# Branch A's ScalarE and VectorE instructions in an order written by hand for all tiles

## The chip, the core and the metric

The kernel runs on one core of one Trainium2 chip. The core's engines are TensorE (PE in the profile, its weight loads PEld), VectorE (DVE), ScalarE (ACT), GpSimd (POOL) and SyncE (SP, which here issues the DMAs). Each runs its own stream of instructions, and they meet at semaphores. The metric is the device time of one execution in microseconds; less is better.

## The reference

One encoder block over 1024 tokens and 16 prepended meta tokens, width 1024: two attention branches side by side, merged by sigmoid gates, then a SwiGLU feed-forward layer. All is float32. Branch A, where the change lies, is differential attention with 4 heads:

```python
s1 = jnp.einsum('bqhd,bkhd->bhqk', q1, k1).astype(jnp.float32) * scale + bias
s2 = jnp.einsum('bqhd,bkhd->bhqk', q2, k2).astype(jnp.float32) * scale + bias
attn = jax.nn.softmax(s1, axis=-1) - lam * jax.nn.softmax(s2, axis=-1)
return jnp.einsum('bhqk,bkhe->bqhe', attn.astype(v.dtype), v)
...
merged = jax.nn.sigmoid(ga) * (y_a @ w_ba) + jax.nn.sigmoid(gb) * (y_b @ w_bb)
```

`bias` is minus the head's slope times the distance of query and key. The gates `ga` and `gb` are two 1024 x 1024 projections of the normed input.

## The kernel before

Every float32 product is made of three matmuls on a high and a low part (`split`, lines 117 and 118: ACT rounds the high part out, DVE or POOL subtracts it to get the low one). Work runs in stages: norm and projections with branch B, then branch A, then the branch outputs, the output projection and the feed-forward layer.

**Branch A** goes over 4 heads of 8 query tiles of 128 rows, 32 tiles in all, numbered `n` from 0 (`h, t = divmod(n, NT)`; the text calls the heads 1 to 4). For each tile there are two maps, first `m = 1`, then `m = 0`, each of 1040 keys in three chunks of 392, 392 and 256 (`scores_a`). So a tile has six chunks: per chunk two matmuls (line 814) into one of five score banks, and one DVE instruction (line 817) that adds the distances, keeps the scores in the map and the running minimum. After a map's third chunk ACT takes the exponential with the sum (line 824). DVE takes the reciprocal of the sum (line 826), POOL scales map 1 by it and by minus lambda (line 828). The join is DVE's `scalar_tensor_tensor` (line 837), map 0 times its reciprocal plus map 1, with a small copy behind it (line 838).

A tile's joined map is turned during the next tile (`T_LAG` is 1): three groups of transposes on TensorE (line 849: four, four and one) into the same five banks, each followed by an ACT copy (line 852) and a DVE subtraction (line 853). Two tiles together go through `values_a` (line 862) in three steps, four tiles through `normed_a`.

**The gates** fill TensorE between these: `gate_steps` has 50 units (products `p` of a Strassen-like scheme, column groups `k`), each of four steps of three matmuls (line 751), in two banks. The result of a unit is added to a kept sum on DVE (line 756) for p = 1, 6 and 7 or copied out on ACT (line 759) for the others, and stored. The first 18 units are all copies. The last 32 take p = 1, 6, 7, 4 in turn, for two k each. The weights of a unit are loaded (`g_load`) and split (`g_split`) three units ahead by `g_ahead`.

**The order.** TensorE's order is by hand (`order_pe`). A string gives the slots of a tile: `s` a chunk, `g` a gate step, `t` a group of transposes of the tile before, `n` a step of values or norm:

```python
SLOTS = "sgsgsngsgsstntnt"
...
for what in SLOTS if n != 1 else "sgsgsngsgssggtntnt":
```

At the start of a head stand more gate steps, 10 (`G_HEAD`), 4 for the first (`G_FIRST`). ACT and DVE are held to program order in tile 0 alone (`order_first`); there, splits wait in `held_back` until `let_go`. From tile 1 on a scheduler with costs of its own orders ACT and DVE. In program order each exponential stands behind its map's last chunk and the join at the end of the tile's slots. POOL and SP are ordered by the scheduler in this stage.

Of the kernel before, what the change touches and what calls it, by code (L numbers as in the profile page):

```python
# [9 lines left out]
F32 = mybir.dt.float32  # L10
# [3 lines left out]
AF = mybir.ActivationFunctionType  # L14
# [5 lines left out]
P = 128  # L20
# [7 lines left out]
AH = 4  # L28
# [8 lines left out]
N_WAIT = 3  # L37
PP2 = 2
# [35 lines left out]
def encoder_block(ctx: ExitStack, tc: tile.TileContext, x, meta, norm_mix, w_in, lq1, lk1, lq2, lk2,  # L74
# [666 lines left out]

    def gate_steps():
        for n, (p, k) in enumerate(order_g):
            g_ahead(n + 1)
            op, act = g_ready.pop((p, k)), G_ACT[p]
            if p in (2, 5, 1):
                g_bank[k] = pp_bank(f"pg{p}_{k}")
            ps = g_bank[k]
            for c in range(4):
                for i, (a, b) in enumerate(((0, 0), (0, 1), (1, 0))):  # L750
                    nc.tensor.matmul(ps, op[:, a, c], quad(b, *act)[:, c], start=(p in (2, 5, 1) and c == 0 and i == 0),  # L751
                                     stop=(p in (2, 3, 4) and c == 3 and i == 2), skip_group_check=True)
                if c == 3:
                    if p in (1, 6, 7):
                        st = g_kept.pop((p, k))
                        nc.vector.tensor_tensor(st, ps, st, ALU.add)  # L756
                    else:
                        st = gpool.tile([P, 512], F32, tag="g", name="gate_stage", bufs=G_BUFS)
                        nc.scalar.copy(st, ps)
                    nc.sync.dma_start(g_place(p, k), st)  # L760
                    if (p, k) in ((5, 3), (5, 7), (3, 7)):
                        later_p = {(5, 3): 6, (5, 7): 7, (3, 7): 4}[p, k]
                        load_sums(later_p, *G_ACT[later_p])
                yield
# [34 lines left out]
    behind_first, n_tile = [], [0]  # L799

    def scores_a(h, t, ld, s):
# [5 lines left out]
        u0 = 896 - t * P  # L807
        for m in (1, 0):
            s[m] = s0s[t % 2] if m == 0 else apool2.tile([P, L], F32, tag="s1", name=f"as1_{nm}", bufs=S_BUFS[1])
            low = far_a  # L810
            for i, (k0, n) in enumerate(A_CHUNKS):
                ps = bank(psum2, "sc", f"aps_{nm}_{m}_{k0}", SC)
                for vv in range(2):
                    nc.tensor.matmul(ps[:, :n], qs[m][:, t * P:(t + 1) * P], ks[m][:, vv, k0:k0 + n],  # L814
                                     start=(vv == 0), stop=(vv == 1))
                far_by = dist_m[:, t] if k0 == last_k0 else dist[:, u0 + k0:u0 + k0 + n]
                nc.vector.tensor_tensor_reduce(s[m][:, k0:k0 + n], ps[:, :n], far_by, slope, low,  # L817
                                               ALU.add, ALU.min, mn[:, m, i:i + 1])
                low = mn[:, m, i:i + 1]
                if i == 1 and behind_first:  # L820
                    behind_first.pop(0)()
                if i < 2:
                    yield
            nc.scalar.activation(s[m][:, 0:L], s[m][:, 0:L], AF.Exp, bias=low, scale=-1.0, accum_out=dn[:, m:m + 1])  # L824
            def scaled(m=m):
                nc.vector.reciprocal(dn[:, m:m + 1], dn[:, m:m + 1])  # L826
                if m:
                    (nc.gpsimd if t % 4 in COMBINE_POOL else nc.vector).tensor_scalar(  # L828
                        s[1][:, 0:L], s[1][:, 0:L], dn[:, 1:2], neglam, ALU.mult, ALU.mult)
            if m and n_tile[0] == 0:  # L830
                behind_first.append(scaled)
            else:
                scaled()
            if n_tile[0] == 0:
                let_go(1)
            yield
        nc.vector.scalar_tensor_tensor(s[0][:, 0:L], s[0][:, 0:L], dn[:, 0:1], s[1][:, 0:L], ALU.mult, ALU.add)
# [79 lines left out]

    for n in range(AH * NT + T_LAG):
        n_tile[0] = n
        if n == 0:  # L920
            order_first = tc.manual_schedule(engines={mybir.EngineType.Activation, mybir.EngineType.DVE})
            order_first.__enter__()
        scoring, turning = iter(()), iter(())
        if n < AH * NT:
# [7 lines left out]
            s = [None, None]  # L932
# [6 lines left out]
        if n >= T_LAG:  # L939
            turning = turn(tiles[n - T_LAG])  # L940
        for what in SLOTS if n != 1 else "sgsgsngsgssggtntnt":
            if what == "s":
                next(scoring, None)
            elif what == "t":
                next(turning, None)
            elif what == "n":
                step_tail()
            else:
                fill(1)
        for _ in scoring:  # L950
            pass
        if n == 0:
            let_go(9)
            held_back = None
            order_first.__exit__(None, None, None)
# [3 lines left out]
        for _ in turning:  # L959
            pass  # L960
# [586 lines left out]
```

## Time and profile before

| | us |
|---|---|
| median of 3 runs (lowest to highest) | 1442.53 (1442.18 to 1443.05) |
| profiled execution, own time | 1443.88 |
| its span, first to last instruction | 1442.1 |
| TensorE busy | 1421.4 |
| VectorE busy | 898.4 |
| ScalarE busy | 679.3 |
| GpSimd busy | 644.5 |
| branch A's score matmuls (line 814), first to last start | 326.0 to 583.7 |

The granted TensorE clock was 0.998 over the span. Times in rows are microseconds from the span's start, durations of one instruction in a group nanoseconds. In a row of the timeline stand the start, the length, the engine, the line, the operation, what it writes and reads, and how many were merged; in brackets the idle time before it and who ended it. A row of a stretch holds, after the stretch and its length, the busy time and count of PE, PEld, DVE, ACT and POOL, the granted clock, the DMA share and GB/s. A row of waits has who waited for whom, the sum, the times and the longest.

### The profile page before, as it was taken

To read this page: it belongs to the slowest core of one execution; us is meant where nothing else is said; L and a number is where in the kernel's file an instruction comes from. 1 tells how busy PE (TensorE), PEld (TensorE's weight loads), DVE (VectorE), ACT (ScalarE), POOL (GpSimd) and SP (SyncE) were. 2 spreads that over 40 slices of the span, in tenths; PEclk is the share of its full clock that TensorE was granted. 3 is DMA by queue.
4 is the path that set the end of the run, shared out by engine and by line. 5 is a ranking of instruction groups with operands and counts; after the bars stand their busy time and mean duration, and the time that the engine had idled before them with its cause. 6 is when DMAs were issued, how large, how long until landed. Compare 5 with 4: busy or idle time off the path is not lost.

```text
span 1442.1 us, 21169 instructions
## 1 busy us (share of the span) xinstructions
PE 1421.4 (99%) x7279; PEld 1219.8 (85%) x7279; DVE 898.4 (62%) x1624; ACT 679.3 (47%) x1290; POOL 644.5 (45%) x605
## 2 busy tenths in 40 slices
PE   8999999999999999999999999999999999999997
PEld 6988989988889989888888788888888888788886
DVE  7468536637787979625514966555555554787567
ACT  6366535546565655545314643333333333444444
POOL 5589227744333433425522775544454442000444
PEclk9999999999999999999999999999999999999999
DMA  8367668996558464586602534333333333964443
GB/s 245 87 211 231 196 160 273 278 286 230 176 177 271 133 220 148 183 258 209 212 22 102 154 99 164 101 105 103 110 100 103 98 109 101 327 207 142 124 129 139
DMA packets 188891, 242.41 MB, mean 168 GB/s; under 512 B 18208, under 2 KB 115936, under 8 KB 188784
## 3 DMA queue, kind: packets, MB, share of 16 engines
q1 hardware_dynamic: 188784, 241.07, 52.9%
q8 instruction: 57, 0.93, 0.3%
q14 instruction: 50, 0.41, 0.1%
HBM read 157.45 MB, written 77.00 MB: 163 GB/s over the span
## 4 chain that ended last, share of the span: by engine, by line
PE 82%; POOL 6%; issue 4%; DVE 4%; DMA 3%; ACT 1%; SPq 0%; POOLq 0%; ACTq 0%; DVEq 0%
PE pg L1328 28%; PE pg L751 8%; PE pd L1422 8%; PE po L1105 6%; PE ppa L796 6%; PE aps L814 4%; PE apy L862 3%; PE pp_qb L214 3%; POOL oa L118 3%; PE pp_ka L214 2%; PE pp_va L214 2%; PE apt L849 2%; PE pp_qa L214 2%; PE bpt L356 1%; PE bpy L362 1%
## 5 line engine op out<-in xcount | busy, mean ns | idle before, releaser
L118 POOL TENSOR_TENSOR wop<-wf,wop 128x512 fp32r<-128x512 f32 x128 | 171.8, 1347 | 166.4 <-ACT wop L117 150.5
L1328 PE MATMUL pg<-t,wop 128*128 128x512 f32 x1056 | 242.6, 389 | 0.0
L1328 PEld LDWEIGHTS pg<-t,wop 128*128 128x128 f32 x1056 | 198.3, 188 | 41.1
L1422 PE MATMUL pd<-ob,oa 128*128 128x512 f32 x924 | 210.7, 390 | 0.8 <-POOL oa L118 0.4
L1422 PEld LDWEIGHTS pd<-ob,oa 128*128 128x128 f32 x924 | 173.2, 188 | 38.2 <-DVE ob L118 1.1
L1328 PE MATMUL pg<-b,wop 128*128 128x512 f32 x792 | 185.6, 392 | 2.4 <-DVE c L1337 2.4
L1328 PEld LDWEIGHTS pg<-b,wop 128*128 128x128 f32 x792 | 149.5, 189 | 34.2 <-issue 2.4
L751 PE MATMUL pg<-hT_hi,gop 128*128 128x512 f32 x384 | 142.3, 395 | 0.0
L118 POOL TENSOR_TENSOR oa<-ra,oa 128x512 fp32r<-128x512 f32 x33 | 44.0, 1336 | 171.2 <-ACT oa L117 169.8
L117 ACT ACTIVATE wop<-wf 128x512 fp32r<-128x512 f32 x128 | 80.2, 631 | 83.2 <-PE pg L1328 48.6
L118 POOL TENSOR_TENSOR gop<-gr,gop 128x512 fp32r<-128x512 f32 x47 | 66.0, 1406 | 106.3 <-ACT gop L117 106.3
L117 ACT ACTIVATE oa<-ra 128x512 fp32r<-128x512 f32 x77 | 48.7, 632 | 106.1 <-PE pd L1422 45.3
L824 ACT ACTIVATE as<-as,amn 128x1040 f32<-128x1040 f32 x64 | 74.5, 1164 | 45.4 <-DVE amn L817 34.4
L1163 DVE TENSOR_TENSOR s<-wf,wf 128x512 f32<-128x512 f32 x22 | 25.5, 1160 | 105.6 <-DMA wf<-in_w_ff_gate_dram 57.7
L814 PE MATMUL aps<-ak,aq 128*128 128x392 f32 (+1 forms) x384 | 89.3, 327 | 1.6 <-DVE amn L817 1.1
L1105 PE MATMUL po<-woh,mT 128*128 128x512 f32 x384 | 88.0, 390 | 0.0
L1105 PEld LDWEIGHTS po<-woh,mT 128*128 128x128 f32 x384 | 71.9, 188 | 14.8
L751 PEld LDWEIGHTS pg<-hT_hi,gop 128*128 128x128 f32 x384 | 72.2, 188 | 11.2 <-DVE gk L756 0.2
L814 PEld LDWEIGHTS aps<-ak,aq 128*128 128x128 f32 x384 | 69.3, 188 | 14.6 <-DVE amn L817 2.0
L343 POOL TENSOR_SCALAR bs<-bs,bdn 128x432 f32<-128x432 f32 (+1 forms) x64 | 41.4, 665 | 85.9 <-DVE bdn L341 74.1
L751 PE MATMUL pg<-hT_lo,gop 128*128 128x512 f32 x192 | 75.8, 395 | 0.0
L828 POOL TENSOR_SCALAR as<-as,adn,neglam 128x1040 f32<-128x1040 f32 x32 | 38.9, 1216 | 57.5 <-DVE adn L826 43.9
(289 smaller groups left out, 3099.4 us busy)
## 6 DMA issues: line engine op xcount, KB each, us to landing
ra<-aop SPq DMA_DIRECT2D x77, 256.0 KB, 2.7
wf<-in_w_ff_gate_dram SPq DMA_DIRECT2D x24, 512.0 KB, 3.9
wf<-in_w_ff_up_dram SPq DMA_DIRECT2D x24, 512.0 KB, 3.9
aop<-as SPq DMA_DIRECT2D x44, 256.0 KB, 2.1
w_c<-in_w_in_dram SPq DMA_DIRECT2D x17, 512.0 KB, 6.1
aop<-c SPq DMA_DIRECT2D x33, 256.0 KB, 2.0
ts_d<-to SPq DMA_DIRECT2D x16, 512.0 KB, 3.8
gw<-in_w_in_dram SPq DMA_DIRECT2D x32, 256.0 KB, 4.1
```

The source lines that it names most:

```text
L117: nc.scalar.activation(hi, src, AF.Copy)
L118: lo_eng.tensor_tensor(lo, src, f32(hi), ALU.subtract)
L214: nc.tensor.matmul(ps[:, :n], a[:, c, :], b[:, c, at:at + n], start=(c == 0 and i == 0), stop=(c == DC - 1 and i == 2))
L343: nc.gpsimd.tensor_scalar(st[:, r, :W], st[:, r, :W], dn[:, r:r + 1], 1.0, ALU.mult, ALU.mult)
L751: nc.tensor.matmul(ps, op[:, a, c], quad(b, *act)[:, c], start=(p in (2, 5, 1) and c == 0 and i == 0), stop=(p in (2, 3, 4) and c == 3 and ...
L796: nc.tensor.matmul(ps, w[:, a, j, :], src(j, b, tk), start=(j == 0 and n == 0), stop=(j == 3 and n == 2))
L814: nc.tensor.matmul(ps[:, :n], qs[m][:, t * P:(t + 1) * P], ks[m][:, vv, k0:k0 + n], start=(vv == 0), stop=(vv == 1))
L824: nc.scalar.activation(s[m][:, 0:L], s[m][:, 0:L], AF.Exp, bias=low, scale=-1.0, accum_out=dn[:, m:m + 1])
L862: nc.tensor.matmul(py[:, cols], v[:kp, a, k, :], at_[:kp, k, b, :], start=(k == 0 and j == 0), stop=(k == 8))
L1105: nc.tensor.matmul(ps, mT[:, c, a, t * P:(t + 1) * P], wos[q, c][:, b], start=(c == 0 and n == 0), stop=(c == DC - 1 and n == 2))
L1328: nc.tensor.matmul(ps, op[:, x, c, :], b[:, y, c, :], start=(p in (1, 2, 5) and c == 0 and n == 0), stop=(p in (4, 2, 3) and c == 3 and n ...
L1422: nc.tensor.matmul(ps[u], oa[:, a, u * P:(u + 1) * P], ob[:, b, :], start=(p in (1, 2, 5) and j == 0 and k == 0), stop=(p in (2, 3, 4) and ...
```

## The change

ACT and DVE are held to program order in all 33 rounds of the tile loop (`order_av` in place of `order_first`), and the program order itself is written anew. The parts of `scores_a` behind the chunks become functions that the loop calls at chosen slots:

- `exp_a(s, 1)` behind the third chunk, as before; `exp_a(s, 0)` behind the first group of transposes (`EXP_AT = 1`), not behind the sixth chunk;
- `scale_a` (reciprocal on DVE, scaling on POOL) behind the fifth chunk;
- `join_a` of tile n - 1 behind the first chunk of tile n (`JOIN_AT = 1`), not at the end of its own tile;
- a gate unit's result (`gate_result`) behind the matmuls of the next gate step;
- splits wait in `held_back` in all tiles; one is let go behind the third chunk and one behind the third group of transposes, more when a unit lacks its own.

TensorE's order is not touched. The diff, cut to its core:

```diff
+JOIN_AT = 1
+EXP_AT = 1
...
+    def gate_result(p, k, ps):
+        if p in (1, 6, 7):
+            st = g_kept.pop((p, k))
+            nc.vector.tensor_tensor(st, ps, st, ALU.add)
+        else:
+            st = gpool.tile([P, 512], F32, tag="g", name="gate_stage", bufs=G_BUFS)
+            nc.scalar.copy(st, ps)
+        nc.sync.dma_start(g_place(p, k), st)
+        if (p, k) in ((5, 3), (5, 7), (3, 7)):
+            later_p = {(5, 3): 6, (5, 7): 7, (3, 7): 4}[p, k]
+            load_sums(later_p, *G_ACT[later_p])
...
             g_ahead(n + 1)
+            while (p, k) not in g_ready:
+                let_go(1)
...
+                while owed:
+                    gate_result(*owed.pop(0))
                 if c == 3:
...
+                    owed.append((p, k, ps))
+                    if n == len(order_g) - 1:
+                        gate_result(*owed.pop(0))
                 yield
...
-            nc.scalar.activation(s[m][:, 0:L], s[m][:, 0:L], AF.Exp, bias=low, scale=-1.0, accum_out=dn[:, m:m + 1])
...
+            s["low", m] = low
             yield
+
+    def exp_a(s, m):
+        dn = s["of"]
+        nc.scalar.activation(s[m][:, 0:L], s[m][:, 0:L], AF.Exp, bias=s["low", m], scale=-1.0, accum_out=dn[:, m:m + 1])
+
+    def scale_a(t, s):
+        dn = s["of"]
+        nc.vector.reciprocal(dn[:, 1:2], dn[:, 1:2])
+        (nc.gpsimd if t % 4 in COMBINE_POOL else nc.vector).tensor_scalar(
+            s[1][:, 0:L], s[1][:, 0:L], dn[:, 1:2], neglam, ALU.mult, ALU.mult)
+
+    def join_a(s):
+        dn = s["of"]
+        nc.vector.reciprocal(dn[:, 0:1], dn[:, 0:1])
         nc.vector.scalar_tensor_tensor(s[0][:, 0:L], s[0][:, 0:L], dn[:, 0:1], s[1][:, 0:L], ALU.mult, ALU.add)
...
+    order_av = tc.manual_schedule(engines={mybir.EngineType.Activation, mybir.EngineType.DVE})
+    order_av.__enter__()
     for n in range(AH * NT + T_LAG):
...
+        if n == AH * NT:
+            join_a(tiles[n - 1][2])
         for what in SLOTS if n != 1 else "sgsgsngsgssggtntnt":
...
+            if what == "s" and n < AH * NT:
+                next(scoring)
+                scored += 1
+                if scored == JOIN_AT and n:
+                    join_a(tiles[n - 1][2])
+                if scored == 3:
+                    exp_a(s, 1)
+                    let_go(1)
+                if scored == 5:
+                    scale_a(t, s)
+                if scored == 6 and n == 0:
+                    exp_a(s, 0)
+            elif what == "t" and n:
+                next(turning)
+                turned += 1
+                if turned == EXP_AT and n < AH * NT:
+                    exp_a(s, 0)
+                if turned == 3:
+                    let_go(1)
...
+    order_av.__exit__(None, None, None)
     n_gates[0] += HOLD
     raw_w = []
     while tail:
         step_tail()
+        let_go(9)
         fill(3)
```

More of the change, by code (lines that the diff above doesn't have):

```diff
@@ L807, in scores_a @@
         u0 = 896 - t * P
+        s["of"] = dn
         for m in (1, 0):
@@ L931, in encoder_block @@
                 at_ = apool3.tile([P, 9, 2, 256], F32R, tag="at", name=f"at{h}_{t}", bufs=AT_BUFS)
-            s = [None, None]
+            s = {}
             tiles.append((h, t, s, at_, ld[2]))
```

44 lines of the change are left out of this document (3 added, 41 removed).

## Prediction

> **What bounds the kernel now.** I read the page's busy shares first, then the busy time by stretch, then who made TensorE wait.
>
> ```profile
> PE 1421.4 (99%) x7279; PEld 1219.8 (85%) x7279; DVE 898.4 (62%) x1624; ACT 679.3 (47%) x1290; POOL 644.5 (45%) x605
> PE 82%; POOL 6%; issue 4%; DVE 4%; DMA 3%; ACT 1%; SPq 0%; POOLq 0%; ACTq 0%; DVEq 0%
> 526.40:583.40 57.00, 57.00 (x365) 52.70 (x364) 49.25 (x147) 34.14 (x64) 20.93 (x18) 1.00 0.51 167
> sum 296.00, PE 292.67 PEld 263.18 DVE 230.98 ACT 174.05 POOL 117.31; mean PE 48.78 PEld 43.86 DVE 38.50 ACT 29.01 POOL 19.55
> PE apt L849 <- DVE as L837: 1.1, 2, 1.0
> PE aps L814 <- DVE amn L817: 1.1, 3, 0.4
> ```
>
> TensorE bounds the kernel: 99% busy, 82% of the chain. The fourth line sums the branch A stage, 323 to 619 us: 292.67 of 296.00 busy, so only 3.33 us of idle can go there; the two largest waits in it are for VectorE. The third line is the fourth head (pieces in the order PE, PEld, DVE, ACT, POOL): PE is never idle, and DVE is busy 49.25 of 57.00, so DVE idles 1.02 us in a mean tile of 7.47 us (that length is read below). The change can therefore win little, and it loses as soon as it asks DVE to idle more than about that per tile.
>
> The order that the scheduler found for DVE and ACT is seen in the timeline around the end of tile 26 (head 4):
>
> ```profile
> 546.74 0.48 DVE L817 CUSTOM_DVE_ANT_0 as<-aps,dist_m,amn 128x256 f32<-128x256 f32 x1
> 547.15 0.69 DVE L756 TENSOR_TENSOR gk<-pg,gk 128x512 f32<-128x512 f32 x1
> 547.75 0.62 DVE L817 CUSTOM_DVE_ANT_0 as<-aps,dist,amn 128x392 f32<-128x392 f32 x1
> 548.52 0.48 DVE L817 CUSTOM_DVE_ANT_0 as<-aps,dist_m,amn 128x256 f32<-128x256 f32 x1
> 548.93 0.08 DVE L817 DVE_READ_ACCUMULATOR2_ANT amn<- 128x1 f32 x1
> 549.23 0.69 DVE L853 TENSOR_TENSOR at<-apt,at 128x512 fp32r<-128x512 f32 x1
> 549.84 0.62 DVE L817 CUSTOM_DVE_ANT_0 as<-aps,dist,far_a 128x392 f32<-128x392 f32 x1
> 550.38 0.16 DVE L826 RECIPROCAL adn<-adn 128x1 f32<-128x1 f32 x1
> 550.64 1.30 DVE L837 SCALAR_TENSOR_TENSOR as<-as,adn,as 128x1040 f32<-128x1040 f32 x1
> 551.86 0.62 DVE L817 CUSTOM_DVE_ANT_0 as<-aps,dist,amn 128x392 f32<-128x392 f32 x1
> 552.41 0.87 DVE L853 TENSOR_TENSOR at<-apt,at 128x512 fp32r<-128x512 f32 x2
> 553.21 0.16 DVE L838 COPY as<-as 128x32 f32<-128x32 f32 x1
> 553.29 0.47 DVE L817 CUSTOM_DVE_ANT_0 as<-aps,dist_m,amn 128x256 f32<-128x256 f32 x1
> ```
>
> ```profile
> 546.94 0.63 ACT L117 ACTIVATE gop<-gr 128x512 fp32r<-128x512 f32 x1 [2.76 <-issue]
> 547.48 1.15 ACT L824 ACTIVATE as<-as,amn 128x1040 f32<-128x1040 f32 x1
> 548.53 0.18 ACT L824 ACTIVATION_READ_ACCUMULATOR as<-as,amn 128x1 f32 x1
> 548.62 0.58 ACT L852 ACTIVATE at<-apt 128x512 fp32r<-128x512 f32 x1
> 549.10 1.16 ACT L824 ACTIVATE as<-as,amn 128x1040 f32<-128x1040 f32 x1
> 550.25 0.75 ACT L852 ACTIVATE at<-apt 128x512 fp32r<-128x512 f32 x2
> ```
>
> ACT already runs what the change prescribes: exponential of map 1 (547.48), copy of the first transposes (548.62), exponential of map 0 (549.10), copies of the other two (550.25). DVE does not. While ACT runs the second exponential (549.10 to 550.25), DVE takes the next tile's first chunk (549.84) and the join (550.64), and only at 552.41 subtracts for the second and third transposes. In the hand order these two subtractions stand ahead of that first chunk, so DVE would stand still from 549.84 until the second copy is done, 550.25 + 0.58 = 550.83: 0.99 us, one tile's whole idle, in every tile.
>
> **The change part by part.** No instruction is added or dropped: only orders, and with them waits, move. I lay out the ring that the hand order closes: next tile's first chunk, join, second and third chunk, exponential, copies, subtractions, next first chunk. Steps are start to start from the rows above.
>
> DVE, first chunk to third chunk: 0.54 (549.84 to 550.38), reciprocal 0.26, join 1.30 to its end since the copy reads it, copy 0.08 (553.21 to 553.29), second chunk 0.55 (551.86 to 552.41): 2.73. From the third chunk's start to its exponential about 0.55 (0.48 and the accumulator's read; the row at 548.52 has 0.58). ACT: exponential 1.14, weight split 0.54, first copy 0.48, exponential 1.15, second copy 0.58 to its end. DVE: the last two subtractions 0.80 (552.41 to 553.21). Together 2.73 + 0.55 + 1.14 + 0.54 + 0.48 + 1.15 + 0.58 + 0.80 = **7.97 us**; where a gate's add falls into it, 0.60 more (547.15 to 547.75), **8.57**. Against it stands what TensorE needs:
>
> ```profile
> 526.38 0.53 PE L814 MATMUL aps<-ak,aq 128*128 128x392 f32 x2
> 533.86 0.60 PE L814 MATMUL aps<-ak,aq 128*128 128x392 f32 x2
> 542.51 0.60 PE L814 MATMUL aps<-ak,aq 128*128 128x392 f32 x2
> 547.29 0.60 PE L849 MATMUL apt<-ident,as 128*128 128x128 f32 x4
> 549.07 0.63 PE L814 MATMUL aps<-ak,aq 128*128 128x392 f32 x2
> 556.26 0.61 PE L814 MATMUL aps<-ak,aq 128*128 128x392 f32 x2
> 526.95 0.63 DVE L817 CUSTOM_DVE_ANT_0 as<-aps,dist,far_a 128x392 f32<-128x392 f32 x1 [2.45 <-PE aps L814]
> L756 DVE TENSOR_TENSOR gk<-pg,gk 128x512 f32<-128x512 f32 x24 | 16.4, 682 | 7.4 <-PE pg L751 5.2 <-DMA gk<-g_d 2.0
> ```
>
> Four tiles take 556.26 - 526.38 = 29.88 us (7.48, 8.65, 6.56, 7.19), 7.47 in the mean. *Heads 2 and 4:* a gate unit ends at the fourth fill slot, its result comes behind the next tile's first chunk, and the split behind the first exponential, in the ring. Head 2 copies on ACT while ACT waits anyway: 7.97, 0.50 over. Head 4 has adds on DVE in three units of four (the 24 adds of the last row lie in the last 32 units): (3 x 1.10 + 0.50) / 4 = 0.95 over. *Heads 1 and 3:* the fill of ten steps shifts the phase by half a unit, the split falls behind the third transposes, out of the ring; then the second exponential waits for DVE's sixth chunk, which waits behind the reciprocal of map 1's sum: 0.55, then 1.05 + 0.18 until that sum is read, 0.16 for the reciprocal and 0.55 for the chunk make 2.49 from third chunk to second exponential, so 2.73 + 2.49 + 1.15 + 0.58 + 0.80 = 7.75, 0.28 over. With an add DVE itself is later there: 0.41 (546.74 to 547.15), add 0.60, two chunks 1.10, 0.16 and 0.55 make 2.82, so 8.08, 0.61 over; three adds in four give head 3 (3 x 0.61 + 0.28) / 4 = 0.53. With six tiles of head 1 and eight of each other: 1.7 + 4.0 + 4.2 + 7.6 = **17.5 us** that DVE falls behind.
>
> TensorE can be ahead by some of it. It has five score banks, so the first transposes (the seventh bank of a tile) need the second chunk's bank back: in the short tile they stand at 547.29 - 542.51 = 4.78 after the first chunk, and DVE frees that bank 2.73 after starting it, so a lag to 2.05 is free; without lag DVE starts 0.57 after TensorE (526.95). Walking head 2 with those lengths: the first tile leaves a lag of 2.0 (there TensorE's transposes still come last), then 1.4, 2.9, and stalls of 0.9, 0, 0.3, 0.5 and 1.5: 3.2 us, only 0.8 under its 4.0, since a long tile's slack is not kept for the next. Taking 0.8 off each head: 17.5 - 3.2 = 14.3 us of new stalls. The ten fill steps at a head (about 7 us of PE alone) let DVE catch up, so no lag crosses heads.
>
> Bounds: below, each head hides the lag of its longest tile, 2 us: 17.5 - 8 = 9.5. Above, nothing is hidden and the two rows of branch norms per four tiles (one multiply of about the add's 0.60) fall in the ring too, 8 x 0.60: 22.3. I take 14.3, as the walk has the trace's own lengths.
>
> *Other edits.* A gate's result one step later (a DVE add or an ACT copy, its store on SP, and in three cases the two loads of later sums) costs nothing: its bank is wanted again only when the other bank's unit of four fill steps is through, so three steps of cover are left; without them it is one step of three 0.232 us matmuls (rows below), 0.70. A held split (ACT copy, POOL subtraction, and the load of a kept sum on SP) is let go at two places a tile, and one is needed: splits stay two units, so two tiles, ahead of TensorE, and their loads and POOL work lie beside that. Without that cover a split is an ACT copy and a POOL subtraction on the path, some 2 us a unit. POOL's scaling of map 1 has a whole turn of transposes before the join wants it. Behind the last tile held splits go out ahead of the fill: nothing.
>
> Gain: at most the stage's 3.3 us of idle, which I grant. Sum: 14.3 - 3.3 = +11.0. The profiled execution took 1443.88 us (span 1442.1 and 1.8 around it), 1.35 above the median of the runs; 1443.88 + 11.0 = 1454.9, on the median **1453.5 us**.
>
> A rule weighed against this cap:
>
> ```profile
> 451.43 6.95 PE pg L751 x30
> L751 PEld LDWEIGHTS pg<-hT_hi,gop 128*128 128x128 f32 x384 | 72.2, 188 | 11.2 <-DVE gk L756 0.2
> ```
>
> Thirty unbroken matmuls take 0.232 us each, with 0.188 of weight load: loads are busy 81% where nothing waits, and 263.18 / 296.00 = 89% in the stage, so the loads show no further idle. The Trainium skill, Perfetto Trace Analysis, Identifying the Most-Contended Engine, says that a busy share of matmuls is a poor measure of headroom and that the share of weight loads is the good one. By it the cap on the gain would be 296.00 - 263.18 = 32.8 us and not 3.3; the unbroken stretch speaks against that.
>
> **The rivals.** *Faster:* the lag never reaches 2.05, because my 0.55 from chunk to exponential and my end-to-start steps are each a little long; it decides in the head's third tile: below a ring of 7.47 no stall comes, and the idle of 3.3 goes: 1439.2. For it: ACT's order is today's, and DVE often takes the first chunk ahead of the join already. Against: 0.5 us per ring is much for such errors. *No change:* the stalls are about the idle won, 3 us, because the five banks hide the lag of each head: 1442.5. It needs a ring within 0.15 of TensorE's tile. The same comes out if the scheduler's order was nearly this one. *Worse on ACT:*
>
> ```profile
> ACT gate_stage L759 <- DMA g_d<-gate_stage: 5.2, 1, 5.2
> ```
>
> Once before, ACT stood 5.2 us behind a gate copy that waited for a store to free its buffer. By hand, exponentials and copies are queued behind it in every tile of heads 1 and 2; two such waits more add 10.4: 1464.
>
> **How the numbers follow.** Forecast 0.60, worse on ACT 0.15, no change 0.10, faster 0.15. Bounds of the forecast are 9.5 - 3.3 = 6.2 and 22.3 over: 1448.7 to 1464.8. The range takes in the faster case's time and the ACT case: 1439 to 1465. A change of 0.2% (2.9 us) is about what can be told here: faster 0.15, within 0.10, slower 0.75.
>
> **What would show it.** Right: DVE's second subtraction at most tiles starts just as ACT's second copy ends, with about 1 us of idle before it; PE gains waits at the first transposes, for DVE's second chunk or join, 10 to 20 us, most in head 4; the four-tile period there is over 32 us; the stretches outside 323 to 619 are unchanged. Wrong: PE's idle in that stretch at or below 3.3 us, or the waits named for gate stores or DMAs.

## The result, and the profile after

The changed kernel takes **1496.49 us** (median of 4 runs, 1495.28 to 1499.52) against 1442.79 for the kernel before: a ratio of 1.0374, with an interval of 1.0356 to 1.0392, or +53.7 us. The forecast was 1453.5 us, with a range to 1465: the sign was right, the size was not. The profiled execution took 1495.94 us, with a span of 1494.2. Lines below are those of the changed kernel: the score matmuls moved from L814 to L826, the scores' chunks on DVE from L817 to L829, the exponential from L824 to L839, the join from L837 to L850, the copy and subtraction of the transposes from L852 and L853 to L865 and L866, the transposes from L849 to L862, the branch norm's square from L869 to L882 and its sums from L875 to L888, the gates' matmuls from L751 to L769, a gate unit's add and copy from L756 and L759 to L749 and L752, the split from L117 and L118 to L119 and L120.

Busy time, and the chain of waits, from the page:

```profile
PE 1443.4 (97%) x7279; PEld 1235.9 (83%) x7279; DVE 906.8 (61%) x1624; ACT 674.0 (45%) x1290; POOL 637.9 (43%) x605
PE 71%; DVE 7%; POOL 7%; issue 6%; ACT 6%; DMA 3%; SPq 0%; POOLq 0%; DVEq 0%; ACTq 0%
```

TensorE's part of the chain fell from 82% to 71%; DVE and ACT, 5% together before, hold 13%. Busy time by stretch (PE, PEld, DVE, ACT, POOL, then the granted clock): the first row is the fourth head with its last score chunks, the second the whole branch A stage.

```profile
566.00:632.00 66.00, 58.93 (x347) 53.72 (x346) 49.10 (x139) 32.54 (x63) 22.01 (x19) 0.92 0.42 136
323.00:672.00 349.00, 314.66 (x1766) 278.10 (x1765) 238.57 (x656) 168.34 (x325) 111.54 (x93) 0.94 0.50 163
```

Before, the fourth head had TensorE busy without a gap at a granted clock of 1.00. Now 7.07 of 66.00 us are idle and the clock is 0.92. All of the loss lies in this stage: the first tile's first score matmul starts at 325.94 us (326.04 before), the last tile's at 631.58 (579.00), 52.6 us later, of 52.1 that the span grew.

Who makes each engine wait (total, times, longest): TensorE first, then DVE and ACT.

```profile
PE apst L888 <- ACT ysq L882: 15.3, 7, 2.3
PE apt L862 <- DVE amn L829: 9.5, 14, 1.3
PE pg L769 <- ACT gop L119: 5.2, 1, 5.2
PE pg L769 <- ACT gate_stage L752: 2.5, 1, 2.5
...
DVE at L866 <- ACT at L865: 48.6, 57, 3.2
...
ACT as L839 <- DVE amn L829: 136.1, 37, 12.6
```

The wait that the forecast rested on is there: DVE's subtractions wait 48.6 us for ACT's copies, 0.85 us in the mean, and TensorE waits at the first transposes in 14 places. But the largest wait of TensorE is another: the branch norm's sums, for ACT's square.

**Where the 52.1 us are.** I measured every distance from one matmul's start to the next and took from it the median distance of the same two shapes before. What is left, in us (they go from start to start, so they differ a little from the waits listed above):

| | before | after |
|---|---|---|
| norm's sums, waiting for ACT's square | 0 | 16.4 (7 places) |
| first transposes, waiting for DVE | 2.1 | 11.7 (14 places) |
| gate matmuls at the starts of heads 2 and 3 | 0 | 8.0 (2 places) |
| score matmuls, waiting for a bank | 2.7 | 3.1 |
| others | 0.6 | 0.3 |
| all matmuls in stretches of half the granted clock | 0 | 18.8 |
| sum | 5.4 | 58.3 |

The difference, 52.9, accounts for the span's 52.1. The last row of the table is distance in excess inside 41.0 us during which the clock was halved; it is not all loss, as an experiment below shows.

**The ring.** DVE's timeline from one tile to the next in head 1:

```profile
358.93 0.60 DVE L829 CUSTOM_DVE_ANT_0 as<-aps,dist,far_a 128x392 f32<-128x392 f32 x1
...
359.72 1.53 DVE L850 SCALAR_TENSOR_TENSOR as<-as,adn,as 128x1040 f32<-128x1040 f32 x1
...
361.38 0.62 DVE L829 CUSTOM_DVE_ANT_0 as<-aps,dist,amn 128x392 f32<-128x392 f32 x1
...
362.15 0.48 DVE L829 CUSTOM_DVE_ANT_0 as<-aps,dist_m,amn 128x256 f32<-128x256 f32 x1
...
366.63 0.88 DVE L866 TENSOR_TENSOR at<-apt,at 128x512 fp32r<-128x512 f32 x2 [0.94 <-ACT at L865]
367.43 0.60 DVE L829 CUSTOM_DVE_ANT_0 as<-aps,dist,far_a 128x392 f32<-128x392 f32 x1
```

From first chunk to next first chunk it is 8.50 us, and within 0.01 us of it in two more plain tiles of head 1 (plain: with no branch norm in it); the two tiles ahead of these take 9.64 and 9.02. It is 8.31 in two tiles of head 2, and 8.9 in most plain tiles of heads 3 and 4. The 0.94 in brackets is the idle time foreseen as 0.99. From first to third chunk it takes 3.22, where the forecast had 2.73.

**The norm's stop.** ACT's and TensorE's timelines in tile 10, head 2:

```profile
424.95 1.16 ACT L839 ACTIVATE as<-as,amn 128x1040 f32<-128x1040 f32 x1 [3.48 <-DVE amn L829]
...
426.11 0.61 ACT L119 ACTIVATE gop<-gr 128x512 fp32r<-128x512 f32 x1
426.63 0.57 ACT L882 ACTIVATE ysq<-apy 128x512 f32<-128x512 f32 x1
...
427.26 1.86 PE L888 MATMUL apst<-ones,ysq 128*128 128x1 f32 x8 [2.32 <-ACT ysq L882]
```

The square at 426.63 needs only the branch output that is long done. It stands behind the exponential of map 1, for which ACT waits idle 3.48 us until DVE has the row minimum. TensorE, whose order is fixed, waits 2.32 us in front of the norm's sums, with more transposes queued behind them. Before, the scheduler had put the same square right behind a copy of transposes, without a wait; the next exponential followed at 412.56:

```profile
408.47 0.60 ACT L869 ACTIVATE ysq<-apy 128x512 f32<-128x512 f32 x1
```

**The starts of heads.** DVE, ACT and TensorE at the start of head 3, tile 16, and at that of head 2:

```profile
483.31 0.69 DVE L749 TENSOR_TENSOR gk<-pg,gk 128x512 f32<-128x512 f32 x1 [6.18 <-DMA gk<-g_d]
487.51 1.16 ACT L839 ACTIVATE as<-as,amn 128x1040 f32<-128x1040 f32 x1 [12.57 <-DVE amn L829]
...
488.68 0.61 ACT L119 ACTIVATE gop<-gr 128x512 fp32r<-128x512 f32 x1
489.34 0.79 PE L769 MATMUL pg<-hT_hi,gop 128*128 128x512 f32 x1 [5.17 <-ACT gop L119]
...
401.09 0.59 ACT L752 COPY gate_stage<-pg 128x512 f32<-128x512 f32 x1 [6.78 <-DMA g_d<-gate_stage]
401.73 0.50 PE L769 MATMUL pg<-hT_hi,gop 128*128 128x512 f32 x1 [2.46 <-ACT gate_stage L752]
```

A gate's add stands 6.18 us for a kept sum's load, with the tile's score chunks queued behind it on DVE; ACT waits 12.57 for those; and the gate's split, queued behind that exponential, reaches TensorE 5.17 late. One DMA wait passes along three engines, because each takes its work in the written order (12.57 is not all due to the load: ACT also had nothing to do during the ten gate steps at the head's start). At head 2 the wait is for the store that frees a staging buffer.

### The profile page after: what moved, and what is told of

Its sections match the earlier page's. It is cut to its first block, busy times and chain, and to the rows that moved or that the text cites. A ratio compares the mean times of both kernels' runs of the same rounds, so it can differ in the third digit from the quotient of the medians.

```text
span 1494.2 us, 21141 instructions
## 1 busy us (share of the span) xinstructions
PE 1443.4 (97%) x7279; PEld 1235.9 (83%) x7279; DVE 906.8 (61%) x1624; ACT 674.0 (45%) x1290; POOL 637.9 (43%) x605
## 4 chain that ended last, share of the span: by engine, by line
PE 71%; DVE 7%; POOL 7%; issue 6%; ACT 6%; DMA 3%; SPq 0%; POOLq 0%; DVEq 0%; ACTq 0%
PE pg L1351 26%; PE pd L1445 8%; PE ppa L809 6%; PE po L1128 5%; PE pg L769 5%; PE pp_qb L216 3%; POOL oa L120 3%; DVE as L829 2%; PE pp_ka L216 2%; PE pp_va L216 2%; ACT as L839 2%; DVE as L850 2%; PE pp_qa L216 2%; PE aps L826 2%; PE bpt L358 1%
## 5 line engine op out<-in xcount | busy, mean ns | idle before, releaser
L120 POOL TENSOR_TENSOR wop<-wf,wop 128x512 fp32r<-128x512 f32 x128 | 172.0, 1349 | 165.6 <-ACT wop L119 153.1
L769 PE MATMUL pg<-hT_hi,gop 128*128 128x512 f32 x384 | 148.4, 411 | 7.8 <-ACT gop L119 5.2
L839 ACT ACTIVATE as<-as,amn 128x1040 f32<-128x1040 f32 x64 | 74.4, 1163 | 136.2 <-DVE amn L829 136.1
L119 ACT ACTIVATE wop<-wf 128x512 fp32r<-128x512 f32 x128 | 80.2, 631 | 84.2 <-PE pg L1351 48.2
L120 POOL TENSOR_TENSOR oa<-ra,oa 128x512 fp32r<-128x512 f32 x33 | 44.0, 1335 | 170.1 <-ACT oa L119 168.6
L120 POOL TENSOR_TENSOR gop<-gr,gop 128x512 fp32r<-128x512 f32 x47 | 60.5, 1290 | 95.6 <-ACT gop L119 95.6
L826 PE MATMUL aps<-ak,aq 128*128 128x392 f32 (+1 forms) x384 | 94.4, 342 | 1.8 <-DVE amn L829 1.3
L119 ACT ACTIVATE oa<-ra 128x512 fp32r<-128x512 f32 x77 | 48.7, 632 | 104.6 <-PE pd L1445 47.3
L769 PEld LDWEIGHTS pg<-hT_hi,gop 128*128 128x128 f32 x384 | 75.8, 197 | 21.1 <-ACT gop L119 5.4
L826 PEld LDWEIGHTS aps<-ak,aq 128*128 128x128 f32 x384 | 73.6, 200 | 15.7 <-DVE amn L829 1.9
L1128 PEld LDWEIGHTS po<-woh,mT 128*128 128x128 f32 x384 | 71.9, 188 | 14.8
L866 DVE TENSOR_TENSOR at<-apt,at 128x512 fp32r<-128x512 f32 (+1 forms) x96 | 50.2, 551 | 48.7 <-ACT at L865 48.6
L769 PE MATMUL pg<-hT_lo,gop 128*128 128x512 f32 x192 | 78.7, 410 | 0.0
```

The source lines that it names most:

```text
L119: nc.scalar.activation(hi, src, AF.Copy)
L120: lo_eng.tensor_tensor(lo, src, f32(hi), ALU.subtract)
L866: nc.vector.tensor_tensor(lo, pt[:lo.shape[0], :nb], f32(hi)[:lo.shape[0]], ALU.subtract)
L1128: nc.tensor.matmul(ps, mT[:, c, a, t * P:(t + 1) * P], wos[q, c][:, b], start=(c == 0 and n == 0), stop=(c == DC - 1 and n == 2))
```

## The experiments

My theory was the forecast's: DVE's wait for ACT's second copy sets a ring longer than TensorE's tile. The rivals were that ACT's queue is the larger cost (the norm's squares behind an exponential that waits), that the held splits and loads are, and that the halved clock is. Microseconds over the kernel before are against its median in the same set of runs (1443.72, 1444.15, 1443.88 or 1444.36); differences from the changed kernel are of the medians as they stand.

**The places, or the one order?** The changed kernel's text, with the hand order ended after the first tile as before, so that the scheduler places everything else:

```
         if n == 0:
+            order_av.__exit__(None, None, None)
...
-    order_av.__exit__(None, None, None)
```

> The changed kernel's program text (new places of joins, exponentials, results, held splits), with ACT and VectorE held to it in tile 0 alone and left to the scheduler from tile 1 on. Theory 'strict order' (the loss is in holding both engines to one order, not in the places): within 5 us of before, 1438 to 1448, clock whole in the stage. Theory 'places' (the later results, held splits and late kept loads cost by themselves): 1455 or more, with the waits at the heads' starts as in the changed kernel.

Measured: 1445.66 us, ratio 1.0013 (1.0001 to 1.0024), +1.5. Of TensorE's waits in the table above the norm's and the heads' are gone, and at the transposes one for a chunk is left, beside two for the join, 1.1 us together, as before:

```profile
PE apt L862 <- DVE amn L829: 1.9, 1, 1.9
```

The new places in the text cost next to nothing as long as the scheduler may move DVE's and ACT's instructions; holding the two engines to them costs the rest. The converse is the kernel before, with its first tile's hand order kept on to the end of the loop:

```
-            order_first.__exit__(None, None, None)
...
+    order_first.__exit__(None, None, None)
```

> The kernel before with its own program order kept by hand on ACT and VectorE for all tiles (the first tile's hold extended to the end of the loop), so joins at the end of their tile, map 0's exponential behind the sixth chunk, results at once. Theory 'any strict order costs': slower than before by over 20 us; against the changed kernel it tells what the new places are worth: with the join ahead of the next first chunk and both exponentials ahead of the copies I expect more waits than in the changed kernel, 1490 to 1530. Theory 'new places are at fault': 1440 to 1465.

Measured: 1541.86 us, ratio 1.0679 (1.0658 to 1.0700), +97.7, more than the 1490 to 1530 expected. Its waits (lines of the kernel before):

```profile
PE apt L849 <- DVE amn L817: 16.1, 26, 1.7
PE aps L814 <- DVE at L853: 14.2, 18, 1.3
PE apst L875 <- ACT ysq L869: 13.0, 7, 2.2
```

The change's text is thus 44 us better than the old text when both are held; but the scheduler's order of either is better by far.

**Which engine's order?** The hand order for DVE alone, then for ACT alone (the other is left to the scheduler):

```
-    order_av = tc.manual_schedule(engines={mybir.EngineType.Activation, mybir.EngineType.DVE})
+    order_av = tc.manual_schedule(engines={mybir.EngineType.DVE})
```

> The changed kernel with VectorE alone held to the program order; ScalarE is left to the scheduler. Theory 'ring' (VectorE, bound to take its subtractions for the second and third transposes ahead of the next first chunk, waits for ScalarE whatever order that one has): first chunk to first chunk stays over 8 us in plain tiles, and only the norm's tiles may get shorter, since the scheduler can take the squares first: 1470 to 1490. Theory 'ScalarE's order': 1450 or less.

> The changed kernel with ScalarE alone held to the program order; VectorE is left to the scheduler. Theory 'ring': VectorE can take the next first chunk and the join while it would wait for a copy, so the plain tiles come down to TensorE's 7.5 us; what is left is the norm's squares behind an exponential: 1446 to 1462. Theory 'ScalarE's order': 1475 or more.

Measured: DVE alone 1477.23 us, 1.0233 (1.0215 to 1.0250), +32.9; ACT alone 1472.98, 1.0194 (1.0178 to 1.0209), +28.6. TensorE's waits, with DVE held:

```profile
PE apt L862 <- DVE amn L829: 13.7, 11, 2.1
PE aps L826 <- DVE amn L829: 4.0, 11, 0.5
```

and with ACT held:

```profile
PE apst L888 <- ACT ysq L882: 12.8, 7, 2.7
PE pg L769 <- ACT gate_stage L752: 3.5, 1, 3.5
```

The division is nearly clean. DVE's order alone makes the waits at the transposes and score banks (and 1.4 us at one gate), and no wait at a norm; ACT's order alone makes the norms' and the gates' waits (8.1 us at gates in all), and none at the transposes. The two sum to 61.5, more than the 53.7 of both together. Neither run is as simple as its theory. With DVE held, its waits for ACT's copies are 19.3 us and not 48.6, and its rings vary from 6.9 to 10.0 us where over 8 in every plain tile was expected: the order costs DVE more than the one wait that the forecast had. With ACT held, 1472.98 lies between the two times expected (to 1462, and from 1475). TensorE's clock was halved for 23.9 us of the stage with DVE held, and for 20.5 with ACT held.

**The norm.** The exponential of map 1 goes behind the norm's first step, so that the square is ahead of it on ACT:

```
-                if scored == 3:
-                    exp_a(s, 1)
-                    let_go(1)
...
                 step_tail()
+                if scored == 3 and n < AH * NT:
+                    exp_a(s, 1)
+                    let_go(1)
```

> The changed kernel, with map 1's exponential and the split issued behind the first norm-or-value step and not ahead of it; nothing else moves. Theory 'queue' (the two ACT steps of the branch norm stand behind an exponential that waits for VectorE, so TensorE's sums of squares wait 15.3 us in 7 places, and the halved clock that follows them costs as much again): those waits fall under 2 us, the halved stretches at tiles 10, 14, 22, 26 and 30 go, and the time falls by 20 to 30 us to 1466 to 1476. Theory 'ring alone' (VectorE's lag is the cause and the squares are only where it shows): the waits move to the next transposes, the time falls by less than 8 us, 1489 or more.

Measured: 1484.02 us, 1.0279 (1.0257 to 1.0301), 12.5 less than the change, between the two theories. ACT's timeline around the tile shown above:

```profile
419.18 0.62 ACT L882 ACTIVATE ysq<-apy 128x512 f32<-128x512 f32 x1
...
422.78 1.16 ACT L839 ACTIVATE as<-as,amn 128x1040 f32<-128x1040 f32 x1 [2.40 <-DVE amn L829]
```

and TensorE's first wait of this kernel:

```profile
PE apt L862 <- DVE amn L829: 15.1, 20, 1.3
```

The norms' waits, 15.3 us, are gone, and the rings of the seven norm tiles shrink from 9.3 to 11.0 us to between 8.50 and 9.13. The time at half clock falls with them, from 41.0 to 13.7 us. The waits at the transposes grow from 9.5 to 15.1: while TensorE stood at a norm, DVE caught up, and now it doesn't. So the norm's queue is the largest single place of those tried, and still less than a quarter of the loss.

**DVE's wait for the second copy.** Two ways to take it away: the second and third subtractions behind the next tile's join, and the second exponential behind the third transposes' copy:

```
-            nc.vector.tensor_tensor(lo, pt[...], f32(hi)[...], ALU.subtract)
+            late_subs.append(sub) if b else sub()
...
                     join_a(tiles[n - 1][2])
+                    while late_subs:
+                        late_subs.pop(0)()
```

> The changed kernel, with VectorE's subtractions for the second and third transposes issued behind the next tile's join and not ahead of its first chunk, as the scheduler had them. Theory 'ring' (VectorE stands still for ACT's second copy in every tile): its 48.6 us of waits for that copy fall under 15 us, TensorE's 9.5 us of waits at the first transposes nearly vanish, the lag that the squares' exponential waits for goes too, and the time falls by 25 to 45 us, to 1450 to 1472. Theory 'queue' (the squares' place on ACT): the waits for them stay above 10 us and the time falls by less than 12 us.

```
-EXP_AT = 1
+EXP_AT = 3
```

> The changed kernel with the exponential of map 0 behind the third transposes' copy (one constant, 1 to 3). Theory 'ring': the second copy no longer waits for an exponential, so VectorE's waits for copies fall by over 25 us; the join waits for the exponential in its place, 0.3 to 1 us a tile; net a fall of 5 to 25 us, 1470 to 1490. Theory 'queue': within 5 us of the changed kernel, since the squares stand where they stood.

Measured: late subtractions 1493.16 us, 1.0341 (1.0322 to 1.0361), too near the change to tell apart; late exponential 1490.33, 1.0319 (1.0292 to 1.0346), 6.2 less. In the second DVE's waits for copies fall from 48.6 to 28.0 us, a smaller fall than the 25 foreseen, and the norms' waits stay at 15.0. In the first (its own lines of the norm are L889 and L895):

```profile
PE apst L895 <- ACT ysq L889: 14.9, 7, 2.3
...
PE aps L826 <- DVE at L866: 5.0, 9, 1.6
...
PE apt L862 <- DVE amn L829: 0.4, 1, 0.4
DVE at L866 <- ACT at L865: 21.2, 29, 2.9
```

The transposes' waits fell from 9.5 to 0.4, as the ring theory says, and DVE's waits for copies to 21.2 (under 15 was expected). The time did not follow: 5.0 us came back at the score banks, whose reader now stands behind the late subtractions, and the norms' waits stayed. The traces add one thing that no theory had. With this edit the small copy behind the join often falls where a split's subtraction runs on POOL, and 13 of the 32 copies took 1.13 us or more in place of 0.18 (rows in the last section), 12.6 us of DVE's time in all. This undoes what was won: the ring in head 1 is 8.23 us in its last plain tiles, and would be some 7.3 without the copy's 0.97 (an estimate), which is under TensorE's 7.47. All nine of the waits at the score banks come behind such a copy, or behind a join held up in the same way. So the run is no clean test of the ring theory; no run kept POOL's work away from the copies.

**Held splits.** After the first tile nothing is held back:

```
+        if n == 0:
+            let_go(9)
+            held_back = None
```

> The changed kernel with the weight splits made at once from tile 1 on (none held back), so that each split and its kept load stand at the first step of the unit three ahead. Theory 'held splits' (at the heads' starts the kept load is issued too late, VectorE waits 6.2 us for it and TensorE 5.2 us for a split): these two waits and the 6.8 us at half clock behind them go, the time falls by 7 to 14 us, to 1482 to 1489. Theory 'loads' (the head's own loads fill the queue, held or not): within 4 us of the changed kernel.

Measured: 1487.44 us, 1.0312 (1.0292 to 1.0332), 9.1 less. The two waits of gate matmuls for ACT at the head starts, 5.2 and 2.5 us, fall to 0 and 0.2, and the pauses there from 8.0 to 2.0, as the theory of the held splits says; the norms' waits stay, and the transposes' (10.5 us):

```profile
PE apst L888 <- ACT ysq L882: 12.7, 7, 1.8
```

**Together.** The first two edits (norm first, late subtractions), then these with the unheld splits:

> The changed kernel with both edits of the first two runs: the norm's first step ahead of map 1's exponential, and the second and third subtractions behind the next join. Theory 'two doors' (the norm's place on ACT and VectorE's wait for the second copy each cost, and either alone leaves the lag to the other): the waits at the transposes and for the squares both fall under 3 us, the halved clock is left at the second and third head's start alone, and the time falls by clearly more than 12.5 + 3 us, to 1450 to 1470. Theory 'VectorE is full' (strict order costs VectorE its slack, wherever the wait shows): the waits move to the score banks, 1475 to 1485.

> The changed kernel with three edits together: the norm's first step ahead of map 1's exponential, the late subtractions behind the next join, and no split held from tile 1 on. Theory 'three queues' (what is left in the run with the first two edits sits at the two heads' starts): the stops at gate steps, 13.2 us there with up to 8.7 us at one place, fall under 3 us, no half clock is left in the stage, and the time is 1455 to 1464. Theory 'strict order costs by itself' (VectorE takes its work in an order that TensorE's five banks cannot cover): some 15 us of short pauses at score banks stay and the time does not go below 1452 whichever waits are taken out; if pauses come back elsewhere, 1465 to 1478.

Measured: two edits 1477.93 us, 1.0240 (1.0219 to 1.0261); three 1469.58, 1.0185 (1.0168 to 1.0201). With two edits the largest wait left is one of 8.7 us for a split at the start of head 3, and 10.0 us stand at the score banks, which with the time speaks for the second theory there. The three do not reach the 1455 to 1464 of 'three queues'. Half of the loss is won back; +25.7 are left. TensorE's waits in the kernel with three edits:

```profile
PE aps L826 <- DVE at L866: 4.2, 11, 0.7
PE apt L862 <- DVE amn L829: 3.8, 9, 1.0
PE aps L826 <- DVE amn L829: 3.5, 10, 0.5
```

What is left in these rows is thirty waits of at most 1.0 us each, beside one of 2.4 at a head's start; two stretches of 3.4 us at half clock remain. In this kernel 16 of the 32 small copies took 1.15 us or more, 15.6 us of DVE's time over their usual 0.18; how much of the +25.7 that makes was not tried. No version that I made beat the kernel before.

**The clock.** In the kernel before, the norm's square is done six times over with the same values, which makes TensorE stop and does nothing else:

```
-        nc.scalar.activation(ysq, py, AF.Square)
+        for _ in range(6):
+            nc.scalar.activation(ysq, py, AF.Square)
```

> The kernel before, with the branch norm's squares taken six times over on ACT in place of once (the same values), so that TensorE waits for them in 8 places with ACT and VectorE still ordered by the scheduler. Theory 'clock' (a stop of TensorE of some 2 us is followed by a stretch at half clock): halved stretches of 3.4 or 6.8 us show behind several of the 8 waits and the time rises by clearly more than TensorE's listed waits, by 20 to 40 us. Theory 'waits alone': the clock stays whole and the time rises by the listed waits, under 18 us.

Measured: 1457.04 us, 1.0090 (1.0067 to 1.0112), +13.3. That is less than the 20 to 40 us of the clock theory, yet the clock did not stay whole. The norm's sums wait in three places (eight were expected), and the stage now has two stretches of 6.8 us at half the granted clock:

```profile
PE apst L876 <- ACT ysq L870: 6.0, 3, 4.0
```

In its profiled execution (1459.65 us, 15.8 over that of the kernel before) the pauses are 14.8 us by the reckoning above, 9.4 more than before, and the excess at half clock is 6.6, together 16.0: here a stop on TensorE is paid a second time, by two thirds. In the changed kernel the opposite was tried: two extra fp32 matmuls of 128x512, whose result is overwritten, keep TensorE busy where it waits for the norm.

```
         pst = bank(psum2, "sc", f"apst_{nm}", SC)
+        for _ in range(2):
+            nc.tensor.matmul(pst, ident, dist[:, 0:512], start=True, stop=True)
```

> The changed kernel with work added: two float32 matmuls of 128x512, whose result is overwritten, on TensorE just ahead of the sums of squares, where it stops 2.3 us in seven places. ScalarE and VectorE are as in the changed kernel, so the waits for the squares end when they ended before; only TensorE is kept busy in them. Theory 'clock' (an idle share of some 1.8 us in a 3.4 us window is what halves the clock): the halved stretches behind those stops go (30 of the 41 us), and the time falls by 8 to 16 us although matmuls were added, 1481 to 1489. Theory 'waits alone': no gain, 1495 or more.

Measured: 1492.61 us, 1.0349 (1.0331 to 1.0368), a difference of 3.9 from the change, within its uncertainty. The added matmuls, the wait behind them, and the transposes' wait:

```profile
L888 PE MATMUL apst<-dist,ident 128*128 128x512 f32 x32 | 15.8, 615 | 0.0
...
PE apt L862 <- DVE amn L829: 14.5, 21, 1.3
...
PE apst L890 <- ACT ysq L882: 1.8, 5, 0.4
```

The half clock shrank from 41.0 to 3.4 us, and the time hardly moved: pauses at the transposes grew from 11.7 to 18.3. So most of what the halved clock seemed to cost here was covered: TensorE worked slowly through time that DVE's ring would have made it wait. That the clock is the main cause is refuted; what was won by keeping it up is 3.9 us, and the interval holds no gain as well. The run is a little unkind to the clock: the added matmuls took 15.8 us and filled 13.5 of the 15.3 us of stops, so some 2 us of them (an estimate from these rows) are work added where TensorE did not stop, at the eighth norm above all.

## Why the prediction was wrong in size

**Right:** the sign; that no work is added and only waits move; that DVE stands still for ACT's second copy (0.94 us a tile against 0.99 foreseen); that this stalls the first transposes (9.6 us of pauses more than before against 14.3 foreseen, 9.5 by the list of waits, at the edge of the 10 to 20 named); that the four-tile period of head 4 exceeds 32 us (36.4 on TensorE, a norm's stop among them); that nothing outside the stage changes. That the transposes' stalls came near the forecast is in part luck: the rings are longer than foreseen, and what this adds is hidden by stops that the forecast did not have, as the run with the norm first shows (15.1 us of these waits).

**Wrong, step by step.** The step that failed is that only DVE's ring was given a price: ACT "already runs what the change prescribes", and the other edits cost nothing. Holding ACT alone cost 28.6 us and holding DVE alone 32.9, where the whole forecast was 11.0; the norms' squares are worth 12.5 of it and the held splits 9.1 by the runs that took them away. The one ring that was priced came out too short as well. Of the forecast's own signs of being wrong, one came in part: 2.5 us of TensorE's waits go back to a gate's store, and 5.2 to a load.

*The ring's length.* 7.75 to 8.57 foreseen, 8.31 to 8.90 measured. Three terms were read from rows in which the scheduler had put other work between dependent instructions. A chunk that takes the minimum of the chunk before it starts 0.77 after it (361.38 to 362.15); my 0.55 was from a chunk to the unrelated subtraction behind it (551.86 to 552.41), although a row quoted there, 547.75 to 548.52, has the 0.77. The join took 1.53 in head 1, not 1.30, and the copy and the chunks wait for it. And in head 1 the second exponential does not wait for DVE's sixth chunk, as foreseen, but for ACT's own queue: the gate's copy of 0.47 stands between the two exponentials. In head 1 this gives 3.22 for 2.73 on DVE, and 2.71 for 2.49 from the third chunk to the second exponential (362.15 to 364.86), nearly all of the 0.75 by which 8.50 exceeds 7.75.

*The norms.* They were only in the upper bound, as one multiply of 0.60 on DVE. What they cost is on ACT: a square behind an exponential that waits for DVE, 15.3 us of waits in seven tiles. I had listed what is queued behind a waiting instruction for DVE and not for ACT, since ACT's order for exponentials and copies was "today's". It was for those two; but in the kernel before TensorE never waits for the norm's square, so the scheduler kept it out of their way. The run with the norm first shows it: 12.5 us.

*Edits priced at nothing.* The third rival, worse on ACT, named the mechanism of the head starts (a gate copy that waits for a store, with the tile's work behind it) and priced two more waits at 10.4. It came beside the forecast and not in place of it: 8.0 us of pauses. The cover that I named for a gate's load and for held splits, "three steps of cover", is cover in the scheduler's order, where a waiting add is passed by; the run without the hold gives back 9.1 us.

*The gain.* The 3.3 us of idle granted did not come: waits at the score banks stood at 3.1 against 2.7.

*The clock.* Not priced at all. Taken by itself it is 18.8 us of excess; the run that kept TensorE busy won 3.9 of them, within its uncertainty.

With the measured rings, and two terms that it did not have, the forecast's sum can be brought near the measured time: (8.50 - 7.47) x 6, (8.31 - 7.47) x 8, 1.41 x 8 and 1.43 x 8 (heads 3 and 4 at 8.88 and 8.90) are 35.6, the norm tiles' longer rings add 10.2, less 3.2 for the free lag: 42.6; the head starts with 8.0 and the clock with some 4 make 54.6, where the span grew 52.1. That is an estimate after the fact: it takes the plain ring for every tile, the norm tiles' rings contain part of the half clock, and by TensorE's pauses only 9.6 us stand at the transposes. So it does not show that the way of reckoning was sound. What it shows is that the numbers the forecast was fed came from an order that the change abolishes.

*Where in the stage.* The stalls at the transposes were to be worst in head 4. They are worst in head 1: 4.1 us in five places from 326 to 390 us, against 2.4 in three from 550 to 632. The run with the norm first, where these waits grow from 9.5 to 15.1, suggests why: in the later heads the norms' stops and the half clock hold TensorE already. The other rivals fell: no ring is below 7.47 but the very first tile's (5.27), so nothing got faster, and the scheduler's order was not nearly the new one, or both kernels would have stood together.

The long joins can be told from the trace: the 17 joins of 1.52 us or more all began while a split's subtraction ran on POOL and ended 1.10 us after it, and the 15 joins of 1.30 all began with none running (rows in the last section). No run took that subtraction away alone, so what this costs in all was not measured.

What stays open: how the +25.7 us of the kernel with three edits divide among its short waits, the copies beside POOL and the remaining half clock, and what DVE's wait for the second copy costs by itself.

## What to carry to other kernels

A hand order for an in-order engine must be judged by every instruction that then stands behind a wait, on each engine held, small ones above all: list for ACT as well as for DVE what is ready and may no longer pass. Take the lengths of a ring from dependent instructions that follow each other directly; rows from a schedule that interleaves other work hide the latency that the hand order will expose. And before holding an order, let the scheduler place the new text: here that alone was within 1.5 us of the kernel before, and whatever is gained or lost by holding is then seen by itself, engine by engine.

## What the runs showed of the hardware

**Half the clock after a stop of 2 us.** Behind the norm's stop in tile 10 the distance of equal matmuls goes from 0.23 us to 0.43; the stretch of 424 to 436 us has a granted clock of 0.72. TensorE's timeline, and that stretch:

```profile
422.86 0.40 PE L769 MATMUL pg<-hT_lo,gop 128*128 128x512 f32 x1
423.09 0.39 PE L769 MATMUL pg<-hT_hi,gop 128*128 128x512 f32 x1
...
430.74 0.63 PE L769 MATMUL pg<-hT_hi,gop 128*128 128x512 f32 x1
431.17 0.63 PE L769 MATMUL pg<-hT_lo,gop 128*128 128x512 f32 x1
```

```profile
424.00:436.00 12.00, 9.47 (x39) 8.34 (x39) 7.91 (x25) 6.57 (x12) 3.48 (x3) 0.72 0.34 117
```

The changed kernel has eight such stretches in this stage, of 3.41 or 6.83 us, and their starts (382.73, 403.21, 427.11 and so on) are whole multiples of 3.41 us apart. In the 3.41 us ahead of them TensorE was idle for 1.81 to 2.76 us, in one for all 3.41; up to 1.68 us of idle was not followed by one in this kernel. The bound is not sharp: in four other kernels (norm first, two edits, three edits, DVE alone) a few windows with 0.48 to 0.97 us of idle were followed by half the clock too. The Trainium skill, TensorE: Matmul & The Clock Gate, What's actually happening, in its table of clock states, has the half clock come after at least one idle window of about 3.4 us; the window's length agrees with these starts, but seven of the eight stretches here came without a window that was idle throughout.

**DVE work that stands until POOL's is done.** In the kernel with late subtractions 13 of the 32 copies of 128x32 on DVE took 1.13 to 1.16 us, where the others took 0.18. Each of the 13 began while POOL ran a subtraction of 128x512 and ended 0.03 to 0.04 us after it; none of the others did. One of them:

```profile
342.97 1.13 DVE L851 COPY as<-as 128x32 f32<-128x32 f32 x1
...
342.57 1.49 POOL L120 TENSOR_TENSOR gop<-gr,gop 128x512 fp32r<-128x512 f32 x1 [1.09 <-ACT gop L119]
```

The copy ends at 344.10, the subtraction at 344.06. In the changed kernel the joins show the same. The one at 359.72, shown above, took 1.53 us beside POOL's subtraction, which ends at 360.15; the second row is a join with none beside it:

```profile
358.86 1.29 POOL L120 TENSOR_TENSOR gop<-gr,gop 128x512 fp32r<-128x512 f32 x1 [1.85 <-ACT gop L119]
...
432.34 1.30 DVE L850 SCALAR_TENSOR_TENSOR as<-as,adn,as 128x1040 f32<-128x1040 f32 x1
```

From the end of the subtraction to the end of the join it is 1.10 us in all 17 such joins of that kernel. A join that was under way when the subtraction began was not slowed: in the kernel with late subtractions the one at 341.63 took 1.30, though POOL started at 342.57. No run tried this by itself.
